# Seven block products instead of eight for the gates and branches of a token-mixer merge

## The chip, the cores and the metric

The kernel runs on one core of a Trainium2 chip. The metric is the device time of one execution in microseconds (us). The kernel before was timed three times: 1023.58, 1023.82 and 1025.4 us, median 1023.82. A further execution was taken by the hardware profiler: 1023.27 us, of which 1021.6 us lie between its first and its last instruction (the span).

Engines are named as in the profile: PE is TensorE (PEld its weight loads), DVE is VectorE, ACT is ScalarE, POOL is GpSimd, SP is SyncE, which issues most DMAs here.

## The reference

One decoder layer over 512 tokens of width 1024, in float32. Cut to what matters:

```python
u = rmsnorm(h, g_mix)
(rq, rk, rv, rgate, dq, dk, dv, dz, db, da, gate_r, gate_d) = split(u @ w_in)
ro = retention(rotary(rq), rotary(rk), rv)            # then normed per head
y_ret = (silu(rgate) * ro) @ w_ret_br                 # 1024 x 1024
do = gated_delta(...)                                 # conv, l2norm, chunked solve, scan; then normed
y_dn = (do * silu(dz)) @ w_dn_br                      # 1024 x 1024
merged = sigmoid(gate_r) * y_ret + sigmoid(gate_d) * y_dn
h = h + merged @ w_o
up = causal_dwconv(rmsnorm(h) @ w_up) + b             # 2 x 2816 columns
a, b = split(up)
h = h + (silu(a) * b) @ w_down
out = rmsnorm(h)
```

The change is about the four matrices of 1024 x 1024 behind `merged`: the two gate parts of `w_in`, `w_dn_br` and `w_ret_br`.

## The kernel before, in words

Every dense product is computed from float32 values that are split in two: a rounded high part (`hi`, type fp32r) and the rest (`lo`). A product is then three matmuls: hi x hi, lo x hi, hi x lo. Weights come from memory in raw blocks of 128 x 1024 floats (512 KB), which SP fetches (`fetch`, DMA lines 232 and 235) into two buffers `wraw`. `weights` then makes the parts: ACT casts the raw block to `whi`, DVE subtracts to get `wlo`. Four pairs of `whi` and `wlo` (`WB = 4`) lie ahead of PE. All engine operations go through a wrapper, so that in the profile every ACT, DVE or POOL operation has line 154, every matmul line 169 and every transpose line 173.

The stages, in order of time:

- **Mixers** (from the start to about 448 us). Dense products of the input rows `u` with the parts of `w_in` (`pk`, `pq`, `pv`, `pr`, `pz`), among which the small products of the mixers are put. The delta mixer has 8 heads in two groups of four. For each group `solve` inverts 64 triangular blocks of 32 x 32: it reads them back from memory (`sa`, line 703), runs 31 steps of two dependent DVE operations each (`xtmp`, `xx`), writes the inverse to memory (`x_dram`) and loads it transposed (`tt`, line 719); PE then builds larger inverses (`pm`) and the scan runs (`psc`). `egb` (line 670) is a row of decays spread over partitions, loaded per head. POOL does small powers (`rsqrt`) for all norms: `rk`, `rq`, `rgn`, `ro`.
- **z gates.** `gate_out` multiplies the mixers' outputs (`roT`, `doT`, transposed: channels on partitions) by a SiLU gate from `pz` and splits them into `rr` and `dd`, 8 tiles of 128 x 512 each.
- **Merge.** For each of 8 channel blocks `c`, PE computes two gates from `u` (`pgate`) and two branches from `dd` and `rr` (`py`), 24 matmuls each (`dense_c`: 8 blocks of depth, three passes); ACT takes the sigmoids; DVE multiplies, adds and splits into `mh`, `ml`, which are already transposed as the next product needs them.
- **`w_o`** (`po`, from 622 us): rows by `dense_r`, residual into `h1`, second norm, transposes (`pt`, line 173).
- **Feed-forward** (`pa`, `pb`, from 668 us), with a convolution over tokens on DVE.
- **Down projection** (`pd`, from 910 us). It is already computed in the form of seven products: the matrix and the activations are cut in quarters, seven sums of quarters are multiplied in place of eight quarter products (Strassen's scheme in Winograd's form), and the results are added. The seven lists of weights need four sums of quarters (`s1` to `s4`). They are made in memory by `presum` on POOL's queue: a DMA copies one quarter to a scratch tensor (line 248), a second DMA adds another quarter to it (line 250, `accum_op=ADD`), 704 KB each, while the feed-forward part runs.

The order of the work on PE, ACT, DVE and POOL is the order in which the program writes the instructions. A small planner (`Order`) sets that order: dense products advance its clock, other work is a set of generators that run when their time has come, with assumed costs for each engine, and `hold` moves the clock until a condition is met. On the chip each engine takes its own list in order and waits only for data and buffers; the planner's times play no part there. SP's list is ordered by the compiler's framework.

```python
P, T, NT, KT, H = 128, 512, 4, 8, 8
PRODUCTS = (("w11", "B11"), ("w12", "B21"), ("s2", "T2"), ("s1", "T1"), ("s3", "T3"), ("s4", "B22"), ("w22", "T4"))
HEAP, HEAP2, RAWB, WB = 64, 17, 2, 4
```

Of the kernel before, what the change touches and what calls it, by code (L numbers as in the profile page):

```python
# [54 lines left out]
KW = NK * 512  # L55
PRODUCTS = (("w11", "B11"), ("w12", "B21"), ("s2", "T2"), ("s1", "T1"), ("s3", "T3"), ("s4", "B22"), ("w22", "T4"))
WD = {"w11": 0, "w12": 1, "w21": 2, "w22": 3}
SUMS = (("s1", "w21", "w22"), ("s2", "w11", "s1"), ("s4", "w12", "s2"), ("s3", "w11", "w21"))


def weight_blocks():
# [12 lines left out]
    for c in range(8):  # L74
        b += [("c", "w_in", GD + c * P), ("c", "w_in", GR + c * P),
              ("c", "w_dn_br", c * P), ("c", "w_ret_br", c * P)]
# [4 lines left out]
    for name, _ in PRODUCTS:  # L81
        b += [("d", name, i, min(2, NK - 2 * i)) for i in range((NK + 1) // 2)]
# [4 lines left out]
NB = sum(b[0] != "d" for b in BLOCKS)  # L87
# [88 lines left out]
def body(nc, tc, ctx, io):  # L176
# [45 lines left out]
    count = dict(fetch=0, split=0, take=0)  # L222

    def fetch():
        i = count["fetch"]
        if i < len(BLOCKS):
            b = BLOCKS[i]
            if b[0] == "d":
                n, own = 512 * b[3], (i - NB) % 4 < 2
                raws[i] = (wp if own else late[0]).tile([P, n], F32, name="wraw" if own else "wraw2",  # L230
                                                        tag="wraw" if own else "wraw2", bufs=RAWB)
                sp.dma_start(raws[i], quarter(b[1])[:, 1024 * b[2]:1024 * b[2] + n])
            else:
                raws[i] = wp.tile([P, D], F32, name="wraw", tag="wraw", bufs=RAWB)
                sp.dma_start(raws[i], io["w"][i])
            count["fetch"] += 1


    sums = {n: dram.tile([P, KW], F32, name=n) for n, _, _ in SUMS}

    def quarter(name):
        return io["wd"][WD[name]] if name in WD else sums[name]

    def presum():
        for n, a, b in SUMS:
            for i in range(4):
                c = ck(i, KW // 4)
                nc.gpsimd.dma_start(sums[n][:, c], quarter(a)[:, c])
                yield 6.0
                nc.gpsimd.dma_start(sums[n][:, c], quarter(b)[:, c], accum_op=ALU.add)  # L250
                yield 8.0

    def weights():
# [6 lines left out]
        raw = raws.pop(i)  # L260
# [7 lines left out]
        yield  # L268
        fetch()
# [46 lines left out]
    def dense_r(pss, x, k0=0, nb=4, last=KT, done=None, groups=(range(NT),), tail=1):  # L316
# [18 lines left out]
        for ts in groups:  # L335
# [4 lines left out]
            for t in ts:  # L340
                for n, part in enumerate(parts[t]):
                    for i in range(nb - tail, nb):
                        block(i, (t,), part)
                        if t == NT - 1 and n == len(parts[t]) - 1:
                            used()
# [761 lines left out]
    def combine(k):  # L1107
# [10 lines left out]
        for n in ("B11", "B12"):  # L1118
            del act_raw[n, k]
# [235 lines left out]
```

## Time and profile before

| what | value | read from |
|---|---|---|
| median of three runs | 1023.82 us | times |
| profiled execution, its own time | 1023.27 us | times |
| its span | 1021.6 us | page |
| granted clock of PE over the span | 0.997 | cores |
| PE busy | 1006.7 us, 99% | page, part 1 |
| DVE busy | 640.6 us, 63% | page, part 1 |
| ACT busy | 463.8 us, 45% | page, part 1 |
| DMA moved | 131.60 MB | page, part 2 |
| chain that ended last | PE 82%, DVE 9%, ACT 4% | page, part 4 |

A row of the profile names its line, engine, operation and tiles (out<-in), the shape, the count, the busy time with the mean in ns, and the idle time of the engine just before it with what ended it. Matmuls overlap one another, so the time from one start to the next says more than a duration. DMA rows give the size of one transfer and the median time from issue to landing.

### The profile page before, as it was taken

What the parts mean: (1) busy time and instruction counts of PE and PEld (TensorE: products, weight loads), DVE (VectorE), ACT (ScalarE), POOL (GpSimd) and SP (SyncE); (2) the same over time, 40 slices, a digit from 0 to 9 for tenths busy, and PEclk for the clock granted to TensorE, in tenths of its full rate; (3) what the DMA queues carried; (4) which work ended last, traced back from release to release, by engine and by line L of the source; (5) the groups of instructions that cost most, each with busy time, mean ns of one, the idle gap of its engine ahead of it and who ended that gap; (6) DMA issues with size and microseconds to landing.
All of it is one profiled execution on the core that took longest, in us unless ns stands there. A gap on an engine that the chain in (4) does not pass through costs nothing.

```text
span 1021.6 us, 13993 instructions
## 1 busy us (share of the span) xinstructions
PE 1006.7 (99%) x5329; PEld 838.5 (82%) x5329; DVE 640.6 (63%) x1224; ACT 463.8 (45%) x956; POOL 77.9 (8%) x100
## 2 busy tenths in 40 slices
PE   8999999999999999999999999999999999999997
PEld 7888778887788886988888888898888888888886
DVE  5777798457777895543333323576655676778785
ACT  5699222475445343742222222444444343356664
POOL 3021100011112000110000000111111000000001
PEclk9999999999999999999999999999999999999999
DMA  5344423211222432094232233368887623246663
GB/s 200 105 119 127 106 83 102 85 64 57 73 74 68 105 111 74 22 282 171 101 103 92 94 103 102 91 195 264 216 240 231 171 100 103 88 129 188 204 189 121
DMA packets 55380, 131.60 MB, mean 129 GB/s; under 512 B 21968, under 2 KB 22288, under 8 KB 55312
## 3 DMA queue, kind: packets, MB, share of 16 engines
q1 hardware_dynamic: 50704, 107.63, 32.8%
q0 software_dynamic: 4608, 23.07, 9.3%
q8 instruction: 42, 0.69, 0.3%
q14 instruction: 26, 0.21, 0.1%
HBM read 127.50 MB, written 26.25 MB: 151 GB/s over the span
## 4 chain that ended last, share of the span: by engine, by line
PE 82%; DVE 9%; ACT 4%; DMA 2%; issue 2%; SPq 1%; POOL 0%; POOLq 0%; DVEq 0%
PE pa L169 12%; PE pb L169 12%; PE pd L169 10%; PE py L169 9%; PE pgate L169 9%; PE pr L169 5%; PE po L169 4%; PE pz L169 4%; PE psc L169 3%; PE pq L169 3%; PE pk L169 2%; DVE wlo L154 2%; PE pv L169 2%; DVE xtmp L154 2%; PE pm L169 2%
## 5 line engine op out<-in xcount | busy, mean ns | idle before, releaser
L154 DVE TENSOR_TENSOR wlo<-wraw,whi 128x1024 fp32r<-128x1024 f32 x182 | 218.6, 1201 | 120.9 <-ACT whi L154 120.4
L154 ACT CAST whi<-wraw 128x1024 fp32r<-128x1024 f32 x182 | 187.9, 1032 | 178.9 <-PE py L169 58.9
L169 PE MATMUL pa<-u2hi,whi 128*128 128x512 f32 (+1 forms) x192 | 71.4, 372 | 0.0
L169 PE MATMUL pa<-u2hi,wlo 128*128 128x512 f32 (+1 forms) x192 | 71.3, 371 | 0.0
L169 PE MATMUL pa<-u2lo,whi 128*128 128x512 f32 (+1 forms) x192 | 71.3, 371 | 0.0
L169 PE MATMUL pb<-u2hi,whi 128*128 128x512 f32 (+1 forms) x184 | 69.9, 380 | 0.0
L169 PE MATMUL pb<-u2lo,whi 128*128 128x512 f32 (+1 forms) x184 | 69.9, 380 | 0.0
L169 PE MATMUL pb<-u2hi,wlo 128*128 128x512 f32 (+1 forms) x184 | 69.9, 380 | 0.0
L154 DVE SCALAR_TENSOR_TENSOR acc<-pb,prm,acc 128x511 f32<-128x511 f32 (+1 forms) x44 | 33.0, 749 | 57.1 <-ACT acc L154 56.4
L169 PE MATMUL pd<-whi,T 128*128 128x512 f32 (+1 forms) x198 | 55.4, 366 | 0.0
L169 PE MATMUL pz<-uhi,whi 128*128 128x512 f32 x128 | 52.6, 411 | 0.0
L169 PE MATMUL pr<-whi,uhi 128*128 128x512 f32 x128 | 52.4, 409 | 0.0
L169 PE MATMUL pz<-uhi,wlo 128*128 128x512 f32 x128 | 50.6, 395 | 0.0
L169 PE MATMUL pz<-ulo,whi 128*128 128x512 f32 x128 | 50.4, 394 | 0.0
L169 PE MATMUL pr<-whi,ulo 128*128 128x512 f32 x128 | 50.0, 391 | 0.0
L169 PE MATMUL pr<-wlo,uhi 128*128 128x512 f32 x128 | 49.9, 390 | 0.0
L169 PE MATMUL pgate<-uhi,whi 128*128 128x512 f32 x128 | 49.8, 389 | 0.0
L169 PE MATMUL pgate<-ulo,whi 128*128 128x512 f32 x128 | 49.8, 389 | 0.0
L169 PE MATMUL pgate<-uhi,wlo 128*128 128x512 f32 x128 | 49.8, 389 | 0.0
L154 DVE SCALAR_TENSOR_TENSOR acc<-pa,prm,acc 128x511 f32<-128x511 f32 (+1 forms) x44 | 33.0, 749 | 19.0 <-ACT acc L154 18.2
L169 PEld LDWEIGHTS pa<-u2hi,whi 128*128 128x128 f32 x192 | 36.2, 189 | 6.3
L169 PEld LDWEIGHTS pa<-u2lo,whi 128*128 128x128 f32 x192 | 36.2, 188 | 6.2
(279 smaller groups left out, 2341.8 us busy)
## 6 DMA issues: line engine op xcount, KB each, us to landing
wraw<-w SPq DMA_DIRECT2D x140, 512.0 KB, 3.5
s<-wd POOLq DMA_DIRECT2D x24, 704.0 KB, 8.3
wraw<-s SPq DMA_DIRECT2D x20, 512.0 KB, 4.2
wraw<-wd SPq DMA_DIRECT2D x15, 512.0 KB, 3.7
s<-s POOLq DMA_DIRECT2D x8, 704.0 KB, 7.2
x<-x SPq DMA_DIRECT2D x8, 256.0 KB, 5.9
gb<-g_dram SPq DMA_DIRECT2D x8, 256.0 KB, 4.0
egb<-e_dram SPq DMA_DIRECT2D x8, 256.0 KB, 3.9
```

The source lines that it names most:

```text
L154: return f(out, *args, **kw)
L169: self.engine.matmul(out, lhsT, rhs, start=start, stop=stop, **kw)
```

## The change

The four matrices of the merge are computed by rows, one after the other (gate of the delta branch, gate of the retention branch, delta branch, retention branch), each in seven products of quarters. Blocks of depth per product are `HK = 4` instead of the 11 of the down projection. Each product has two accumulators of 128 rows x 512 columns and uses two weight blocks of 1024 columns; one weight block now serves 12 matmuls.

What is added: the quarter sums of all four matrices, 16 scratch tensors made by 32 DMAs on POOL's queue (128 x 2048 floats each) that the planner places from its time 40 on, 9.5 apart, in the mixers. Sums of the activations: `combine` makes four quarter sums per tile with four DVE operations of 256 columns; for the input rows POOL first adds `uhi` and `ulo` again. Splits of these operands (`parts_of`, `part_of`) run on ACT and DVE while the matrix before is multiplied, started by product numbers (`since`). Results of some products are copied out of PSUM by ACT (`copied`), others are combined with the copy by DVE (`ended`), then gate and branch are joined (`gate_end`, `branch_end`). Since the merged rows now have tokens on partitions, each of 8 tiles is transposed by PE (`m_out`) and split.

What is removed: the 768 matmuls of the old merge (672 take their place), and the split in `gate_out`, which now leaves its product unsplit. `fetch` may use up to four raw buffers from the merge on (two more in space that the mixers leave). `w_o` takes its first column half in two groups of rows, rows 256 to 511 first. The sums for the down projection are now 16 copies first and then 16 additions, placed 7.0 apart.

```diff
-SUMS = (("s1", "w21", "w22"), ("s2", "w11", "s1"), ("s4", "w12", "s2"), ("s3", "w11", "w21"))
+SUMS = (("s1", "w21", "w22"), ("s3", "w11", "w21"), ("s2", "w11", "s1"), ("s4", "w12", "s2"))
...
+    def presum(s, parts, gap):
+        n = 512 * INNER[s] // parts
+        for add in range(2):
+            for name, a, b in SUMS:
+                for i in range(parts):
+                    c = ck(i, n)
+                    if add:
+                        nc.gpsimd.dma_start(sums[s, name][:, c], quarter(s, b)[:, c], accum_op=ALU.add)
+                    else:
+                        nc.gpsimd.dma_start(sums[s, name][:, c], quarter(s, a)[:, c])
+                    yield gap
...
+    def presums():
+        for s in range(DOWN):
+            yield from presum(s, 1, 9.5)
+    spawn(presums(), 40.0)
...
+    def combine(raw, k, nk, y, z):
+        b11, b12 = halves(raw[k])
+        b21, b22 = halves(raw[k + nk])
+        (t3, t1), (t2, t4) = halves(y), halves(z)
+        vec.tensor_tensor(t3, b22, b12, ALU.subtract)
+        vec.scalar_tensor_tensor(t2, t3, -1.0, b11, ALU.mult, ALU.subtract)
+        vec.tensor_tensor(t1, b11, b12, ALU.subtract)
+        vec.scalar_tensor_tensor(t4, t2, -1.0, b21, ALU.mult, ALU.subtract)
...
     def gate_out(...):
         vec.tensor_tensor(sz, sz, src.pop(c), ALU.mult)
-        hi, lo = S(f"{name}h{c}", F32R), S(f"{name}l{c}", F32R)
-        yield
-        yield from split(hi, lo, sz)
+        raw[c] = sz
...
+    def u_raw():
+        for k in (0, 4, 1, 5, 2, 6, 3, 7):
+            uu[k] = S(f"ur{k}")
+            pool.tensor_tensor(uu[k], uhi[k].bitcast(F32), ulo[k].bitcast(F32), ALU.add)
+            yield 3.0
+            if k >= HK:
+                combine_c(uu, "u", k - HK)
...
-    for c in range(8):
-        for _ in range(2):
-            ps = dense_c(u, "pgate")
-            sg = S2("sg")
-            spawn(sigmoid(sg, ps))
-        for x in (dd, rr_):
-            pys.append(dense_c(x, "py"))
-        spawn(merge(c, sgs, pys))
-    hold(lambda: not order.tasks)
+    def all_operands():
+        yield from operands_c(u_opnd, None, "u", 1.2, (0, 0, 0, 0))
+        yield from operands_c(d_opnd, dd, "d", 2.0, (8, 9, 12, 13))
+        yield from operands_c(r_opnd, rr_, "r", 2.0, (16, 18, 20, 21))
...
+    def m_out(t, i, r):
+        yield 0.2
+        pt = transpose4(r, "pmt")
+        yield
+        hi, lo = S(f"mh{t}{i}", F32R), S(f"ml{t}{i}", F32R)
+        yield from split(hi, lo, pt)
+        mh[t, i], ml[t, i] = hi, lo
...
+    def branch_end(s, t, i, r, ps):
+        g = gates[s - 2].pop((t, i))
+        if ps is None:
+            vec.tensor_tensor(r, r, g, ALU.mult)
+        else:
+            vec.scalar_tensor_tensor(r, ps, -1.0, g, ALU.mult, ALU.mult)
+        if s == 2:
+            merged[t, i] = r
+            return
+        vec.tensor_tensor(r, r, merged.pop((t, i)), ALU.add)
+        yield
+        yield from m_out(t, i, r)
+
+    def matrix(s, opnd):
...
+        A, C = ([PS("py") for _ in range(2)] for _ in range(2))
+        prod(0, [[(full, A[t], True, copied(t, 0, A[t]))] for t in range(2)])
+        prod(1, [[(full, C[t], True, ended(t, 0, C[t], ALU.add))] for t in range(2)])
+        prod(2, [[(full, A[t], False, copied(2 + t, 0, A[t]))] for t in range(2)])
+        E = [PS("py") for _ in range(2)]
+        prod(3, [[(full, E[t], True, copied(2 + t, 1, E[t], -1.0))] for t in range(2)])
+        prod(4, [[(full, A[t], False, ended(2 + t, 1, A[t], ALU.subtract))] for t in range(2)])
+        prod(5, [[(full, E[t], False, ended(2 + t, 0, E[t], ALU.add))] for t in range(2)])
+        prod(6, [[(full, A[t], False, only(t, 1, A[t]))] for t in range(2)], tail=1)
+
+    for s, opnd in enumerate((u_opnd, u_opnd, d_opnd, r_opnd)):
+        matrix(s, opnd)
+    spawn(presum(DOWN, 4, 7.0))
...
-        dense_r([PS("po") for _ in range(NT)], m, done=o_done(i), groups=((0, 1), (2, 3)) if i else (range(NT),))
+        dense_r([PS("po") for _ in range(NT)], m_tile, done=o_done(i), groups=((0, 1), (2, 3)) if i else ((2, 3), (0, 1)))
```

`product` is the loop of the down projection made general: for each weight block and each of two row tiles it issues the three passes, and it starts what follows (`copied`, `ended`, `only`) when the accumulators are complete.

More of the change, by code (lines that the diff above doesn't have):

```diff
@@ L221, in body @@
     raws, ready = {}, {}
-    count = dict(fetch=0, split=0, take=0)
+    count = dict(fetch=0, split=0, take=0, plain=0)
+    free = {"wraw": RAWB, "wraw2": 0}
     def fetch():
-        i = count["fetch"]
-        if i < len(BLOCKS):
-            b = BLOCKS[i]
[L228 to L232, printed above, removed]
-            else:
-                raws[i] = wp.tile([P, D], F32, name="wraw", tag="wraw", bufs=RAWB)
-                sp.dma_start(raws[i], io["w"][i])
-            count["fetch"] += 1
@@ L239, in body @@
[L239 to L251, printed above, removed]
+        while count["fetch"] < len(BLOCKS) and any(free.values()):
+            tag = "wraw" if free["wraw"] else "wraw2"
+            free[tag] -= 1
+            i = count["fetch"]
+            count["fetch"] += 1
+            b = BLOCKS[i]
+            n = 512 * b[4] if b[0] == "q" else D
+            raw = (wp if tag == "wraw" else late[0]).tile([P, n], F32, name=tag, tag=tag, bufs=RAWB)
+            if b[0] == "q":
+                sp.dma_start(raw, quarter(b[1], b[2])[:, 1024 * b[3]:1024 * b[3] + n])
+            else:
+                sp.dma_start(raw, io["w"][count["plain"]])
+                count["plain"] += 1
+            raws[i] = raw, tag
@@ new lines, in body, with quarter @@
+    sums = {(s, n): dram.tile([P, 512 * INNER[s] + 64], F32, name=f"{n}_{s}") for s in range(5) for n, _, _ in SUMS}
+    def quarter(s, name):
+        if name not in WD:
+            return sums[s, name]
+        return (io["wd"] if s == DOWN else io["wm"][s])[WD[name]]
+    def presum(s, parts, gap):
[9 more added lines that the diff above has]
+                    yield gap
@@ L268, in weights @@
         yield
+        free[tag] += 1
         fetch()
@@ L325, in block @@
             whi, wlo = blocks[i]
-            hold(lambda: x[1][k0 + 2 * i + 1] is not None)
+            hold(lambda: all(x(k0 + 2 * i + kk, t) for t in ts for kk in range(2)))
             for t in ts:
@@ L452, in body, with u_tile @@
     u_ready = set()
+    def u_tile(k, t):
+        return uhi[k][:, ck(t)], ulo[k][:, ck(t)]
     def u_split(hf, k, pt):
@@ L1211, in body, with down @@
     done = [0] * NT
[L1213 to L1216 removed]
+    def down(p, accs, tail=0):
         at[0] = p
[L1218 to L1253 removed]
@@ L1264, in fifth @@
+    down(1, [[(full, C[t], True, into(t, 0, C[t], ALU.add, last=True))] for t in range(2)])
+    down(2, [[(full, A[t], False, into(2 + t, 0, A[t], ALU.add))] for t in range(2)])
+    down(3, [[(full, E[t], True, into(2 + t, 1, E[t], ALU.subtract))] for t in range(2)])
     def fifth(t):
```

266 lines of the change are left out of this document (158 added, 108 removed).

## The prediction, made before the changed kernel was run

> **What bounds the kernel now.** I read the page's head first, then busy time by stretches, then the instructions of the merge's tiles, then the waits of TensorE.
>
> ```profile
> span 1021.6 us, 13993 instructions
> ```
>
> PE's busy share has modelled ends and proves little; the instructions of the two merge tiles do. These are the first and the last group of the stage (minimum, median and maximum in ns, then first and last start):
>
> ```profile
> L169 PE MATMUL pgate<-uhi,whi x128: 389/389/389, 448.3 to 610.8; 128*128 128x512 f32 x128
> ```
> ```profile
> L169 PE MATMUL py<-rrh,wlo x64: 389/389/389, 465.1 to 622.1; 128*128 128x512 f32 x64
> ```
>
> Gates and branches are 6 groups of 128 or 64, 768 matmuls in all (3x128 + 6x64). From 448.3 to the last start at 622.1 are 767 steps: 173.8 / 767 = 0.2266 us each. No duration differs from 389 ns, so nothing interrupts the stage: **the matmul count sets its 174 us.** The table by stretches (PE, PEld, DVE, ACT, POOL busy in us with counts, clock, DMA share, GB/s) shows how the other engines stand in it, and in three other stages that matter below:
>
> ```profile
> 120.00:140.00 20.00, 19.32 (x92) 15.14 (x91) 19.55 (x38) 3.15 (x3) 0.00 (x0) 1.00 0.21 68
> ...
> 340.00:360.00 20.00, 20.00 (x90) 16.55 (x89) 19.25 (x40) 7.98 (x11) 0.00 (x0) 1.00 0.31 101
> ...
> 380.00:400.00 20.00, 17.74 (x154) 12.92 (x153) 10.63 (x25) 6.50 (x13) 0.00 (x0) 0.91 0.35 103
> 500.00:520.00 20.00, 20.00 (x90) 16.57 (x89) 6.41 (x8) 5.05 (x7) 0.00 (x0) 1.00 0.31 106
> ...
> 700.00:720.00 20.00, 20.00 (x90) 16.55 (x89) 11.43 (x15) 7.46 (x11) 2.72 (x4) 1.00 0.89 251
> 940.00:960.00 20.00, 20.00 (x90) 16.57 (x89) 17.77 (x31) 13.97 (x28) 0.00 (x0) 1.00 0.62 179
> ```
>
> In the merge (500 to 520) DVE is busy 6.41 of 20 us. In the two triangular solves of the mixers (120 to 140, 340 to 360) it is busy 19.3 to 19.6: there DVE is the scarce engine. The down projection (940 to 960), which already has the form that the merge gets, runs PE at full pace (90 matmuls in 20 us) with DVE at 17.77.
>
> **Part 1, fewer matmuls.** Each of four matrices becomes 7 products of 4 blocks x 2 row tiles x 3 passes, 168 matmuls, so 672 instead of 768. They are of the down projection's shape, whose pace the last row above shows to be the same. 96 x 0.2266 = **21.8 us less**.
>
> **Part 2, new transposes.** The merged rows must be turned before `w_o`: 8 tiles of 4 transposes. The nearest row is in the chain of waits (start, length):
>
> ```profile
> 674.36 1.91 PE pt L173 x16
> ```
>
> 0.12 us each, 32 of them: **3.8 us more**, all on PE. Bounds: 2 (some fall in a wait) to 5.
>
> **Part 3, DVE and ACT in the merge.** Weight blocks rise from 32 to 56, each a cast on ACT and a subtraction on DVE; each now feeds 12 matmuls (2.72 us) instead of 24. Operand splits move here from the z gates, and sums of operands, row ends and signs are new. DVE overlaps neighbours, so I price by start-to-start times, from the timeline of DVE in the down projection:
>
> ```profile
> 925.04 1.22 DVE L154 TENSOR_TENSOR wlo<-wraw,whi 128x1024 fp32r<-128x1024 f32 x1
> 926.18 0.68 DVE L154 TENSOR_TENSOR h<-h,pd 128x512 f32<-128x512 f32 x1
> 926.78 1.22 DVE L154 TENSOR_TENSOR wlo<-wraw,whi 128x1024 fp32r<-128x1024 f32 x1
> 927.91 1.09 DVE L154 TENSOR_TENSOR T<-z,T 128x256 fp32r<-128x256 f32 x3
> 928.92 1.22 DVE L154 TENSOR_TENSOR wlo<-wraw,whi 128x1024 fp32r<-128x1024 f32 x1
> ```
>
> So 1.14 us for 1024 columns, 0.60 for 512, 0.335 for 256. DVE then has 56 weight blocks (63.8), 40 splits of 512 (24.0), 8 of 256 (2.7), 32 quarter sums for the two branches (10.7), 24 combinations with PSUM (14.4), 16 products with a gate (9.6) and 8 additions (4.8): 130 us in a stage of 672 x 0.2266 = 152 us, 86%. On ACT:
>
> ```profile
> L154 ACT CAST whi<-wraw 128x1024 fp32r<-128x1024 f32 x175 | 183.5, 1049 | 173.0 <-PE py L169 58.9 <-PE pr L169 40.9 <-PE pd L169 22.6
> ...
> L154 ACT ACTIVATE sg<-pgate 128x512 f32<-128x512 f32 x16 | 9.6, 598 | 56.9 <-PE pgate L169 56.9
> ```
>
> 56 casts of 1.05, 80 operations of 512 at 0.6, 8 short ones: near 111 us, 73%. Neither exceeds the stage, and the down projection bears 89% of DVE without a wait. But the load is uneven. In the third matrix (the first branch) the operands of the fourth are made as well. At its fifth product, 5.44 us long, DVE gets two weight blocks (2.3 us) and about 2.6 rounds of quarter sums and splits (2.0 us each): 7.5 us. At the sixth, two weights, four row-end operations (2.4) and 1.4 rounds: 7.5. At the seventh, 6.3. The backlog goes 2, 4, 5 us. A weight block may be late by 3 x 2.72 = 8.2 us (four buffers) less cast, subtraction and hand-overs, about 5.4; a PSUM tile that the next matrix reuses must be read within 5.4, and is read after 5 + 1.2. **I take 1.5 us**; bounds 0 (DVE keeps up as at 940) to 6 (11% of idle within DVE's queue, as at 940, over matrices two to four: 107 us of work / 0.89 = 120, against 114).
>
> **Part 4, the hand-over to `w_o`.** Before, the last channel's merge needs four DVE operations. Now `w_o` starts with rows 256 to 511, whose last half ends with product six; only product seven (5.44 us) covers the way: two row tiles each need a combination, a gate product, an addition and a split on DVE (8 x 0.60 = 4.8), two weight blocks pass between them (2.3), the pair of product five leaves 4.8 + 2.3 - 5.4 = 1.7, plus transposes (0.5) and a cast (0.6): 9.9. PE waits up to 4.5 us; without backlog or weights, 0.5. Behind it DVE holds `w_o`'s splits, whose first blocks are ready. A wait also has an after-effect here. TensorE's worst wait in mid-kernel, and the matmuls just after it (start, duration):
>
> ```profile
> PE pm L169 <- DMA tt<-x_dram: 2.3, 2, 1.2
> ```
> ```profile
> 388.16 0.63 PE L169 MATMUL pz<-uhi,whi 128*128 128x512 f32 x1
> 388.59 0.63 PE L169 MATMUL pz<-ulo,whi 128*128 128x512 f32 x1
> ...
> 390.29 0.63 PE L169 MATMUL pz<-uhi,wlo 128*128 128x512 f32 x1
> ```
>
> After 2.3 us of waiting they start 0.43 apart, near half pace, until 390.3 (granted clock 0.91 in that stretch): about 7 x 0.2 = 1.4 us on top. So the hand-over costs 0.5 to 5.9; I take **4**, near the upper end because DVE's queue is full there. [...]
>
> **Part 5, the sums of weights during the mixers.** 32 transfers of 1.05 MB on POOL's queue, 16 of them accumulating. Their price and their neighbours:
>
> ```profile
> q0 software_dynamic: 4608, 23.07, 9.3%
> ...
> wraw<-w SPq DMA_DIRECT2D x140, 512.0 KB, 3.5
> s<-wd POOLq DMA_DIRECT2D x24, 704.0 KB, 8.3
> ...
> egb<-e_dram SPq DMA_DIRECT2D x8, 256.0 KB, 3.9
> ...
> sa<-a_dram SPq DMA_DIRECT2D x4, 128.0 KB, 4.8
> ```
>
> 0.093 x 1021.6 / 23.07 = 4.1 us of all 16 engines per MB, 4.3 per transfer. Weight loads bear this: in the feed-forward part (700 to 720, DMA 0.89) PE holds full pace. What does not is the head of each solve; in the chain of waits stands, at the first:
>
> ```profile
> 109.27 5.01 DMA egb<-e_dram
> ```
>
> `egb` is issued behind `sa`, and DVE waits for it. And POOL's queue runs ahead of its plan, since it waits for data only:
>
> ```profile
> 105.49 1.01 POOL L154 TENSOR_TENSOR rq<-ssqq,mhalf 128x4 f32<-128x4 f32 x1 [1.71 <-DVE ssqq L154]
> ```
> ```profile
> 332.52 1.01 POOL L154 TENSOR_TENSOR rq<-ssqq,mhalf 128x4 f32<-128x4 f32 x1 [5.38 <-DVE ssqq L154]
> 422.96 1.01 POOL L154 TENSOR_TENSOR ro<-mso,mhalf 128x4 f32<-128x4 f32 x1 [89.44 <-DVE mso L154]
> ...
> 436.51 0.76 POOL L248 DMA_DIRECT2D s<-wd  x1
> ```
>
> The last row is a sum of the down projection, whose place in the program is behind the merge's last matmul (622.1); it left 186 us earlier, as soon as POOL's work ahead of it was done. So behind each group's last `rq` the next six to ten sums leave as fast as their dependences allow, and one or two lie beside `sa` and `egb`. Each 1.05 MB in flight can hold a small transfer by up to 4.3 us; half of that, 2, is nearer to what a bulk neighbour does to a weight load. DVE, busy 97%, cannot win it back, and TensorE then waits. First solve 2 (0 to 8); second 1, since the low halves of the eight z gates (8 x 0.60) leave DVE in 340 to 380 but the order of work, planned with DVE's costs, closes up accordingly (from -3.7, the whole present stall of 2.3 + 1.4, to 8). **3 us** together. A sum that waits for the sum before it also holds POOL's small powers queued behind it, 0 to 2 us four times, off the path while dense matmuls are left. [...]
>
> **Part 6, at no cost.** Eight additions on POOL rebuild the input rows; POOL is idle from 333.5 to 423, as the row above shows, and even 1 to 2 us each would fit; without that cover they would delay the first gate operands by up to 16 us. The early sums of the down projection, up to five at about 437, compete with block loads of 0.52 MB per 2.72 us; eight blocks (four split, four raw, 21.8 us) cover that; otherwise 0 to 3.
>
> **Sum.** Against the profiled execution's own 1023.27 us (span 1021.6 and 1.7 around it): -21.8 + 3.8 + 1.5 + 4 + 3 = -9.5, so 1013.8; the median of the runs is 0.55 above the profiled time: **1014.4 us.**
>
> **Rivals.** *Nothing waits* (0.18): DVE keeps up as at 940, the hand-over costs 0.5 and the solves gain or lose little: 1023.8 - 21.8 + 3.8 + 0.5 and -3 to +1, 1003 to 1007. For it: PE's pace at 940; against it: Part 4's arithmetic. *DVE becomes the bound* (0.12): 6 in place of 1.5, hand-over at 5.9: 1020 to 1022, perhaps 1017. Against it: 86% on average. *The solves are starved* (0.12), the other side: transfers of sums beside `sa` and `egb` hold DVE's queue at the head of both solves. With 8 us each: 1023.8 - 21.8 + 3.8 + 1.5 + 4 + 16 = 1027; slower from 12.5 us of loss on. For it: POOL's run-ahead and DVE at 97%; against it: weight loads that live beside two bulk transfers at 700. *The change gives nothing* (0.06): the count falls but every stall comes at its middle and the solves take 12: 1022 to 1026.
>
> **Numbers.** My forecast, 1008 to 1020, has 0.52. About 0.2% (2 us) is what a measurement can tell from no change. Faster than 1021.8: 0.52 + 0.18 + 0.09 = 0.79; within: 0.03 + 0.06 = 0.09; slower: 0.12. The range of 8 in 10 is 1003 to 1025.
>
> **What would show it.** Matmuls of the new merge tiles 0.2266 apart, 672 of them. A wait of 2 to 5 us of PE on the split of the merged rows before the first `po`, with starts 0.43 apart behind it. DVE at 17 or more of 20 us in the third matrix, few waits of PE there. `sa` and `egb` landing in 6 to 8 us instead of 4 to 5. I am wrong if PE waits for weights in the merge, if the solves start over 5 us late, or if the hand-over shows no wait.

## The result, and the profile after

The changed kernel took 1054.26 us (median of four runs, 1053.83 to 1055.54), the kernel before beside it 1023.99: a ratio of 1.0295, 95% interval 1.0277 to 1.0313. It is 30 us slower; 1014.4 had been forecast, with 1003 to 1025 as the range of 8 in 10.

Head of the page and queue table of the changed kernel, and first and last starts of tiles (in this kernel the wrapper's line is 160, every matmul has 175, every transpose 179; SP fetches weights in 243 and 245, POOL issues copies in 267 and accumulating transfers in 265):

```profile
span 1053.8 us, 14233 instructions
...
q0 software_dynamic: 9216, 56.63, 21.5%
```
```profile
L175 PE MATMUL pr<-wlo,uhi x128: 387/389/628, 100.7 to 236.4; 128*128 128x512 f32 x128
L175 PE MATMUL pz<-uhi,wlo x128: 387/389/794, 347.4 to 488.7; 128*128 128x512 f32 x128
L175 PE MATMUL py<-whi,uhi x48: 389/389/389, 489.0 to 559.0; 128*128 128x512 f32 x48
L175 PE MATMUL po<-whi,mh x64: 389/389/628, 648.8 to 699.0; 128*128 128x512 f32 x64
```

The same starts for each kernel (us; the rows above are single ones of a tile's three passes; in the table a first start is that of the first pass, the last `pr` that of the second, the last `pz` that of the third; the first solve runs beside `pr`, the second beside `pz`; kernels are named by the labels of the experiments below):

| kernel | `pr` first, last | `pz` first, last | `po` first | `pa` first | span |
|---|---|---|---|---|---|
| before | 99.4, 217.5 | 328.0, 448.1 | 622.4 | 667.7 | 1021.6 |
| after | 100.4, 236.4 | 347.0, 488.7 | 648.8 | 699.7 | 1053.8 |
| e1, no transfers | 100.3, 218.6 | 329.2, 451.2 | 611.2 | 662.1 | 1015.8 |
| e10, e1 and `w_o` turned | 100.1, 218.4 | 328.9, 450.2 | 608.6 | 655.6 | 1009.2 |
| e9, paced wide | 107.9, 228.3 | 339.8, 461.3 | 623.9 | 670.8 | 1024.5 |
| e11, eight in the merge | 101.9, 225.4 | 344.1, 470.7 | 634.2 | 681.1 | 1034.8 |
| e12, later additions | 101.8, 225.7 | 337.1, 463.7 | 629.4 | 676.3 | 1029.9 |
| e17, 16 transfers | 100.8, 221.0 | 332.4, 454.5 | 641.5 | 688.4 | 1042.0 |
| e18, clear of solves | 107.1, 224.7 | 336.7, 460.9 | 622.7 | 669.6 | 1023.3 |

Before to after: first solve 118.1 to 136.0, middle (last `pr` to first `pz`) 110.5 to 110.6, second solve 120.1 to 141.7, merge (last `pz` to first `po`) 174.3 to 160.1, `w_o` 45.3 to 50.9, the rest 353.9 to 354.1. The mixers lose 40.6 us, merge and `w_o` gain 8.6.

The waits of PE in the changed kernel (total us, times, longest), and landing times of the small loads (KB, median us):

```profile
PE pm L175 <- DMA tt<-x_dram: 10.9, 2, 10.3
PE prqT L179 <- DVE qrot L160: 5.9, 1, 5.9
PE prkT L179 <- DVE krot L160: 5.2, 1, 5.2
PE pz L175 <- DVE wlo L160: 5.0, 1, 5.0
PE pvt L179 <- ACT v L160: 3.2, 1, 3.2
PE po L175 <- DVE ml L160: 3.0, 1, 3.0
...
PE py L175 <- DVE ol L160: 2.5, 2, 1.6
```
```profile
egb<-e_dram SPq DMA_DIRECT2D x8, 256.0 KB, 7.3
...
sa<-a_dram SPq DMA_DIRECT2D x4, 128.0 KB, 11.7
```

Before, the longest such row of the mixers was `tt` with 2.3 us, and `egb` and `sa` landed in 3.9 and 4.8. What lies around the first solve, in the timelines of POOL, SP and DVE (start, duration, in brackets the idle time before and what ended it):

```profile
111.23 1.01 POOL L160 TENSOR_TENSOR rq<-ssqq,mhalf 128x4 f32<-128x4 f32 x1 [1.71 <-DVE ssqq L160]
112.19 0.88 POOL L265 DMA_DIRECT2D s<-s  x1
122.06 0.81 POOL L265 DMA_DIRECT2D s<-s  x1 [8.99 <-DMA s<-s]
122.59 2.36 POOL L267 DMA_DIRECT2D s<-wm  x4
```
```profile
112.02 6.04 SPq L781 DMA_DIRECT2D sa<-a_dram  x2
118.17 3.25 SPq L748 DMA_DIRECT2D egb<-e_dram  x1
...
354.24 11.36 SPq L245 DMA_DIRECT2D wraw<-w  x1
```
```profile
125.60 0.69 DVE L160 TENSOR_TENSOR q<-q,egb 128x512 f32<-128x512 f32 x1 [11.34 <-DMA egb<-e_dram]
```

POOL's queue runs ahead right behind `rq`, as forecast: two sums that accumulate and four copies. `sa` is issued at 112.0, beside the first of them, `egb` behind it at 118.2, and DVE stands 11.3 us for `egb`. At the second solve the issue of one weight load took 11.4 us on SP. All of DVE's waits for small loads, after and then before:

```profile
DVE q L160 <- DMA egb<-e_dram: 26.0, 5, 11.3
DVE xtmp L160 <- DMA sa<-a_dram: 10.1, 1, 10.1
...
DVE ta L160 <- DMA tt<-x_dram: 3.2, 3, 2.7
```
```profile
DVE q L154 <- DMA egb<-e_dram: 5.7, 1, 5.7
DVE ta L154 <- DMA tt<-x_dram: 3.0, 3, 2.5
```

So DVE stands 30 us longer for `egb` and `sa`, the loads at the heads (7.9 of them for three `egb` between 60 and 110 us, the rest at the two solves), and as long as before for `tt`, the load at the ends. PE's wait of 10.3 us for `tt` stands at the end of the second solve, and is the lateness of its head. No transfer of sums leaves from 372 us to the end of the solve, and in the chain of waits there the inverse goes out and comes back fast:

```profile
412.22 3.09 DMA x_dram<-xx
...
416.65 1.66 DMA tt<-x_dram
```

ACT stood long for raw weight blocks (16.6 us before):

```profile
ACT whi L160 <- DMA wraw<-w: 81.2, 17, 12.7
```

### The profile page after: what moved, and what is told of

It is laid out like the page before. It is cut to its first block, busy times and chain, and to the rows that moved or that the text cites. A ratio compares the mean times of both kernels' runs of the same rounds, so it can differ in the third digit from the quotient of the medians.

```text
span 1053.8 us, 14233 instructions
## 1 busy us (share of the span) xinstructions
PE 1003.0 (95%) x5265; PEld 834.3 (79%) x5265; DVE 716.8 (68%) x1344; ACT 510.3 (48%) x1028; POOL 112.2 (11%) x140
## 3 DMA queue, kind: packets, MB, share of 16 engines
q0 software_dynamic: 9216, 56.63, 21.5%
## 4 chain that ended last, share of the span: by engine, by line
PE 77%; DVE 10%; DMA 6%; ACT 3%; SPq 2%; issue 2%; POOL 0%; POOLq 0%; ACTq 0%
PE py L175 12%; PE pa L175 11%; PE pb L175 11%; PE pd L175 10%; PE pr L175 6%; PE pz L175 4%; PE po L175 4%; DMA egb<-e_dram 3%; PE psc L175 3%; DVE wlo L160 3%; PE pk L175 2%; PE pq L175 2%; PE pv L175 2%; DVE xtmp L160 1%; PE pm L175 1%
## 5 line engine op out<-in xcount | busy, mean ns | idle before, releaser
L160 ACT CAST whi<-wraw 128x1024 fp32r<-128x1024 f32 x206 | 213.4, 1036 | 223.8 <-DMA wraw<-w 81.2
L160 DVE TENSOR_TENSOR wlo<-wraw,whi 128x1024 fp32r<-128x1024 f32 x206 | 247.7, 1203 | 55.6 <-ACT whi L160 55.0
L175 PE MATMUL py<-whi,ol 128*128 128x512 f32 x160 | 62.5, 390 | 2.5 <-DVE ol L160 2.5
L175 PE MATMUL py<-whi,oh 128*128 128x512 f32 x160 | 62.7, 392 | 0.3 <-ACT oh L160 0.3
L175 PE MATMUL py<-wlo,oh 128*128 128x512 f32 x160 | 62.3, 390 | 0.0
L175 PE MATMUL pz<-uhi,whi 128*128 128x512 f32 x128 | 54.9, 429 | 0.0
L175 PE MATMUL pr<-whi,ulo 128*128 128x512 f32 x128 | 50.9, 397 | 0.0
L175 PEld LDWEIGHTS pa<-u2hi,wlo 128*128 128x128 f32 x192 | 36.2, 189 | 6.2
```

Source lines behind the costliest of these rows:

```text
L160: return f(out, *args, **kw)
L175: self.engine.matmul(out, lhsT, rhs, start=start, stop=stop, **kw)
```

## The experiments

"Before" runs beside every group; their medians were 1022.8 to 1023.5. Where an interval is given it is of the ratio to these. e2, e3, e4 and e8 were executed once each. e1, e3, e8 and e10 load plain quarters in place of sums: their work is the same, their values are not the reference's.

**1. Whose loss is it?** e1 takes the transfers out, e2 puts them into the kernel before, e3 keeps them but for their bytes.

```diff
 # e1: no transfers; in the merge a plain quarter in place of each sum
-    spawn(presums(), 40.0)
 # e2: the kernel before, with the 32 transfers, whose sums nobody reads
+    spawn(msum(), 40.0)
 # e3: as e1, the 32 transfers kept, 64 of 2048 columns
-    nc.gpsimd.dma_start(sums[s, name][:, c], ...)
+    nc.gpsimd.dma_start(sums[s, name][:, :64], ...)
```

> Leaves out the 32 transfers that make the sums of weights during the mixers; where a sum would be loaded, a plain quarter is loaded instead, so the four matrices are computed from wrong weights, with the same number of loads, splits and matmuls. Theory (the transfers crowd out the loads of the mixers): the last z-gate matmul comes back from 488.7 to 448 +- 4 us, and the time is about 1054 - 40 = 1014 us (1010 to 1018). Rival (the new work on ACT, DVE and POOL in the z gates, and the changed order, make the mixers late): the last z-gate matmul stays beyond 470, the time beyond 1035.

> The kernel before, with only the 32 transfers added at the same places in POOL's queue; nothing reads their sums. Theory (crowding): the mixers end about 40 us later than before's 448.1, the time is about 1060 (1050 to 1070). Rival (z-gate work and order): within 5 us of 1024.

> The changed kernel with all 32 transfers cut to 64 of 2048 columns, and plain quarters loaded in place of the sums (wrong weights, same work). POOL's queue keeps its 32 issues and their order, 1/32 of the bytes move. Theory (bytes crowd out loads): as without sums, 1010 to 1018. Rival (POOL's queue: issue time of the transfers and powers queued behind transfers that wait): still over 1030.

Measured: e1 1017.98 (ratio 0.9964, 0.9946 to 0.9983), e2 1057.11, e3 1019.27. The transfers cost 36.3 us in the changed kernel (1054.26 - 1017.98) and 34 in the kernel before, whose solves lack the new work; with 3% of the bytes they cost 1.3, within the spread of e1 (1017.43 to 1022.61). So it is their bytes, not their issues, and not the z gates. In e2 the loss of 33 us lies in the mixers too (last `pz` at 481.2). The other parts together gain 4.9 us.

**2. Which transfers, and what do they hold up?** e4 puts each sum directly behind its copy. e8 has only six copies, 19% of the bytes, three behind the last `rq` of each group. e5 releases each transfer by a small POOL operation (`tick`) that reads a freshly made weight part, one per weight block, with none near `sa` and `egb`. It was to leave out the ends of the solves too, but the blocks chosen for them (27 to 30, 51 to 53) came after the ends.

```diff
 # e4
+    for name, a, b in SUMS:
+        nc.gpsimd.dma_start(sums[s, name][:, c], quarter(s, a)[:, c])
+        nc.gpsimd.dma_start(sums[s, name][:, c], quarter(s, b)[:, c], accum_op=ALU.add)
 # e8 (no other transfers, plain quarters as in e1)
+    if h % GH == GH - 1:
+        for name in ("s1", "s3", "s2"):
+            nc.gpsimd.dma_start(sums[h // GH, name][:, :2048], quarter(h // GH, "w11"))
 # e5, in weights()
+    QUIET = {*range(14, 19), *range(27, 31), *range(41, 47), *range(51, 54)}
+    if todo and i >= 4 and i not in QUIET:
+        pool.tensor_tensor(tick, lo[:, :4].bitcast(F32), mhalf, ALU.add)
+        todo.pop(0)()
```

> The changed kernel with the 32 transfers in pairs: each copy directly followed by its addition, as the kernel before does for the down projection. All bytes still move; an addition waits for its copy, so at most two to three transfers are in flight where POOL has nothing else to wait for, instead of four to six. If the burst matters (how many are in flight at once): the mixers lose about half, 15 to 25 us of the 40, time 1032 to 1042. If only the bytes matter: 1050 to 1058.

> The changed kernel without the 32 transfers (plain quarters are loaded, wrong weights, same work), but with six copies of 1.05 MB, three issued directly behind the last power of q of each group, that is beside the loads at the head of each solve. 19% of the copied and added bytes. If place decides: 10 to 20 us over the 1018 of the version without sums. If bytes decide: 7 us (6/32 of 37). If only additions hurt: within 2 us.

> The changed kernel with the same 32 transfers, each issued only after a small POOL operation that reads the low part of a freshly split weight block, at most one per block, and none for the blocks split around the heads of the two solves and their ends. All bytes move in the mixers as before, but POOL cannot run ahead. Theory (it is the place and the burst): the mixers lose 0 to 8 us against the version without sums instead of 37, time 1018 to 1028. Rival (the bytes alone cost the time): 1045 to 1057.

Measured: e4 1042.91, e8 1037.72, e5 1048.6 (1.0248, 1.0228 to 1.0268). e8 is the telling one: a fifth of the bytes makes over half of the loss, 19.7 us over e1, when it lies at the heads. e4 gives back 11.3 us with all bytes and the same row length, so it also matters how the transfers follow one another; that may be their number at once or their shifted places. e5 missed its forecast, and its time lies where "the bytes alone" had been expected, which e9 and e18 below refute; in e5 `sa` and `egb` landed in 5.2 us, and other small loads were hit, as its waits of PE show:

```profile
PE pm L175 <- DMA tt<-x_dram: 17.4, 2, 9.1
PE pkt L179 <- ACT k L160: 8.9, 1, 8.9
```

`tt<-x_dram` is the inverse coming back at the end of each solve; here it is late itself (11.6 us at the first solve against 2.9 at most before), with transfers leaving at 183 and 186 us beside it. The wait for `k` is ACT standing 6.7 us for `gb<-g_dram`, near 64 us. So there are three places: `gb` (45 to 75 us), the heads of the solves, and their ends.

**3. The hand-over to `w_o`.** e6 is e5 with the first half of `w_o` taking depth blocks 4 to 7 first, whose operands are ready, and 0 to 3 last. e10 is e1 with the same turn. e7 moves the quarter sums of the two branches from DVE to POOL, on top of e6.

```diff
 # e6, e10
-        b += [("r", "w_o", 2 * i, o) for i in range(4)]
+        b += [("r", "w_o", 2 * i, o) for i in ((0, 1, 2, 3) if o else (2, 3, 0, 1))]
 # e7
-        combine(raw, c, HK, y, z)
+        (combine if x == "u" else combine_pool)(raw, c, HK, y, z)
```

> As the paced version, and in the first half of the output product the depth blocks are taken in the order 4 to 7, then 0 to 3, so that it starts with the merged columns that are ready first. Theory (the wait of 3.0 us on the merged split and the half clock behind it are what the hand-over costs): 3 to 6 us faster than the paced version. Rival (DVE's backlog is what costs, the wait only moves to the second two blocks): within 1 us of it.

> The changed kernel without the 32 transfers (the plain quarter is loaded in place of each sum, so the values of the merge are those of other weights) and with w_o's first half in the turned order: the floor for any placing of the transfers. By the hand-over theory the turned order takes away the wait for the split of the merged rows, 3 us, and the half-clock starts behind it, 1 to 2: 1013 to 1015 against 1018.0 without the turn. If the wait only moves to the second pair of row tiles: 1017 to 1018.

> As the version before (paced, turned), and the quarter sums of the two branch operands are made by POOL, six operations of 256 columns, instead of four on DVE: DVE loses 32 operations, 10.7 us of its load in the second and third matrix. Theory (DVE's full queue in the third matrix causes the waits of 2.5 us there, the half clock behind them and part of the hand-over): 2 to 5 us faster than the version before. Rival (latency of the chain, not load): no difference beyond 1 us, or slower by 1 to 3 if POOL delays the operands.

Measured: e6 1044.17 (1.0198, 1.0171 to 1.0224), e10 1010.87 (0.9891, 0.9864 to 0.9918), e7 1056.36. In both turned kernels the wait for `ml` is gone, and `po` has no half-speed matmuls any more (longest 478 ns in both, 628 in the changed kernel). In e10:

```profile
L175 PE MATMUL po<-whi,mh x64: 389/389/478, 608.6 to 654.9; 128*128 128x512 f32 x64
```

By the table, merge and `w_o` together take 210.9 us in e1 and 205.4 in e10: the hand-over cost 5.5 (7.1 by the medians of e1 and e10, 4.4 by those of e5 and e6). e7, 12 us slower than e6, shows that DVE was not to be relieved that way: PE waited 7.4 us for `ol` instead of 2.5 and 3.7 for `oh` instead of 0.3. Nor did the waits for `ol` have half-speed matmuls behind them, which the theory named: behind the longest of the changed kernel, 1.65 us, the starts are 0.33 and then 0.23 us apart.

**4. Can all 32 be placed?** e9 keeps e6's scheme with quiet blocks at all three places. e11 moves the two transfers still ahead of `gb` and eight others into the merge. e12 lets the last sum of each matrix follow four transfers later. e18 clears both solves, takes matrices in pairs, and lets some blocks release two.

```diff
 # e9
-    QUIET = {*range(14, 19), *range(27, 31), *range(41, 47), *range(51, 54)}
+    QUIET = {*range(7, 10), *range(13, 19), *range(23, 27), *range(41, 46), *range(48, 54)}
 # e11 (e12: also 54, and every fifth block of the merge)
+    SLOTS = {4, 10, 11, 12, *range(19, 23), *range(27, 41), 46, 47, *range(60, 92, 4)}
 # e18
+    SLOTS = {**dict.fromkeys((3, 4, 12, *range(30, 41), 54, 55, 57, 61, 65, 69, 73, 78, 83, 88), 1),
+             **dict.fromkeys((10, 11, 32, 34, 36, 38), 2)}
```

> All 32 transfers stay and are released one per new weight block, as in the two paced kernels before, and w_o's first half takes its depth blocks in the turned order. But now no transfer is released beside any of three kinds of small load that a waiting engine needs at once: gb (blocks 7 to 9), the heads of both solves (13 to 18, 41 to 45) and the x_dram loads at the ends of both solves (23 to 26, 48 to 53). 14 of them leave in the middle region, 220 to 340 us, where the changed kernel carried 14 at no loss. Theory 'it is the place' (a transfer costs only what it holds up of a small load that an engine is waiting for): the mixers give back nearly all, pz ends at 450 to 458 instead of 482.3, and the time is 1012 to 1022, under the kernel before. Rival 'it is the bytes' (each transfer costs about 1 us wherever it lies): 1035 to 1048, as the paced kernels.

> The wider paced kernel before this lost 16 us to the floor without transfers (1010.9): 7.8 of them between 44 and 108 us, where two transfers leave 4 us ahead of g_dram and gb; 2.1 and 1.0 around the first solve's end; 4.1 in the merge, where four transfers left in its first 25 us beside its first weight blocks. Here those two and those four move: 24 transfers stay in the mixers (block 4, blocks 10 to 12, 19 to 22, 27 to 40, 46 and 47), and the last matrix's 8 leave during the merge, one per four weight blocks (10.9 us), where the profile without transfers shows the 16 DMA engines busy 0.56 and weights eight blocks ahead. Theory 'it is the place': 1012 to 1018, below the kernel before (1023.3). Rival 'the merge pays': eight transfers of 4.3 us beside weight loads hold up weights or TensorE there by over 5 us: 1019 to 1027. If the gb wait comes from something else than the two transfers: 1022 or more, with pr again first at 107.

> The kernel before this had the gb wait gone (pr first at 101.9 instead of 107.9), but four sums that accumulate on a sum only just issued stood on POOL's queue for 3.5 to 7.9 us (147, 159, 271, 379 us), with POOL's small powers behind them (TensorE then waited 3.4 for ro), and in the merge eight transfers and the five run-ahead sums of the down projection filled the DMA engines from 520 to 580. Here the last accumulation of each matrix goes four transfers later, so that no transfer waits for the one just before it; 25 transfers stay in the mixers and 7 leave in the merge, one per five weight blocks (13.6 us); the down projection's sums are held until the merge's last blocks. Theory 'place, and POOL's queue behind a waiting sum': first solve back to 120, second to 121, merge 158 to 160: 1014 to 1020. If the queue matters little and the bytes beside the solves decide, the solves keep their 123 and 126: 1024 to 1030.

> All 32 transfers whole (8 KB rows), none now between 100 and 200 us nor between 330 and 420 us: two leave near 30, five at 77 to 90, fifteen between 200 and 325 (four blocks release two), two near 430, and eight in the merge, one per four to five weight blocks. Matrices take turns in pairs, so that no sum follows directly on the one it adds to. Against the last placing of all 32 (1025.2) the first solve should come back from 123.6 to 118 or 119 between the first and last product of its dense stage, the second from 126 to 121, and the merge stay 5 to 7 us above its 146. By 'misplaced transfers' 1013 to 1020, below the kernel before. If the fuller middle (DMA engines some 0.8 busy) now delays gb or POOL's powers there: 1022 to 1030.

Measured: e9 1027.05 (1.0035, 1.002 to 1.0049), e11 1032.95 (1.0096, 1.0069 to 1.0122), e12 1025.19 (1.0015, 1.0004 to 1.0026), e18 1022.47 (0.999, 0.9979 to 1.0001). Place, order and turn are worth 32 us at equal bytes, from 1054.3 to 1022.5, some 4 to 7 of them by the turn. But each forecast below the kernel before was missed, and e18 cannot be told from it. e9 lies between its two theories. e11 did take the loss ahead of the first `pr` away (101.9 instead of 107.9), so the two transfers ahead of `gb` were its cause. It lost 8 us in the middle (118.7), where one accumulating transfer stood 7.9 us on POOL's queue at 271 us, 5 in each solve (123.5 and 126.6), and 5 in the merge, with eight transfers in it (163.5 against 158.4 in e10). e12 took the loss in the middle away (111.4); its solves stayed (123.9 and 126.6), as its rival had it, and so did its merge (165.7). The profiles of e12 and e18 are of their slowest executions, 6.5 and 2.6 us above the medians. What e18 still loses against e10 is 14.1 us of span: 7.0 before the first `pr`, 1.5 in the middle, 2.9 in the second solve, 3.3 in merge and `w_o`. Some of its stretches and a wait (columns as in the prediction), and the first `pr` of e12:

```profile
80.00:100.00 20.00, 20.00 (x104) 16.86 (x103) 14.68 (x26) 15.32 (x38) 5.65 (x9) 1.00 1.00 277
100.00:120.00 20.00, 17.64 (x86) 14.71 (x85) 9.13 (x19) 11.26 (x36) 3.69 (x5) 0.91 0.75 209
...
400.00:420.00 20.00, 18.41 (x176) 14.82 (x175) 9.81 (x29) 7.64 (x29) 0.00 (x0) 0.83 0.12 44
```
```profile
PE pkt L179 <- ACT k L160: 2.4, 1, 2.4
```
```profile
L175 PE MATMUL pr<-whi,uhi x128: 389/389/775, 101.8 to 225.4; 128*128 128x512 f32 x128
```

Two blocks released two transfers each near 80 to 90: the DMA engines stand at 1.00 there, PE loses 2.4 us in the next stretch, and its clock falls from 1.00 to 0.91; e12, with three transfers there instead of five, reaches `pr` 5.3 us earlier. About 1 of these 5.3 was there by 69 us, where e18 had one transfer more near 30 (`pk` at 68.7 against 67.6). The first solve itself is then free of loss (117.6). In 400 to 420 no transfer runs (DMA 0.12), and PE still lost: at 402.0 it had waited 1.6 us for ACT's copy of `tt` (0.9 in e10), and that stretch's clock is 0.83. What makes ACT late there is not settled.

**5. How does a transfer hold up a small load?** e13 and e14 are the changed kernel with each transfer cut along its columns into four or eight, so rows of 2 and 1 KB in place of 8 KB.

```diff
-            yield from presum(s, 1, 9.5)
+            yield from presum(s, 4, 2.375)
```

> The changed kernel with each of the 32 transfers cut along its columns into four, each of 128 rows of 2 KB instead of 8 KB: same bytes, same place in the program, four times the issues on POOL (0.55 us each, 53 us more of an idle POOL). Theory 'whole rows in turn' (a small load waits at each of its packets for a whole row of a transfer): sa and egb land in about half the time, 6 to 8 us instead of 11.7 and 9, and the loss of 37 us shrinks by half or more: 1030 to 1042. Rival 'bytes ahead' (a small load waits for what is already queued, whatever its cut): 1050 to 1060, landing times as in the changed kernel. If short rows make the transfers themselves dearer (more than 4.3 us of all engines per MB): above 1060.

> The same with eight pieces of 1 KB rows (224 more issues on POOL). 'Whole rows in turn': sa and egb at 5 to 6 us and 1025 to 1036, below the kernel with 2 KB rows. 'Bytes ahead': 1050 to 1065.

Measured: e13 1039.89 (1.0153, 1.0116 to 1.019), e14 1054.32 (1.0294, 1.0257 to 1.0331). Landing of `egb` and `sa`, e13, e14, and e4 with its rows of 8 KB:

```profile
egb<-e_dram SPq DMA_DIRECT2D x8, 256.0 KB, 4.8
sa<-a_dram SPq DMA_DIRECT2D x4, 128.0 KB, 8.2
```
```profile
egb<-e_dram SPq DMA_DIRECT2D x8, 256.0 KB, 5.1
sa<-a_dram SPq DMA_DIRECT2D x4, 128.0 KB, 6.2
```
```profile
egb<-e_dram SPq DMA_DIRECT2D x8, 256.0 KB, 5.1
...
sa<-a_dram SPq DMA_DIRECT2D x4, 128.0 KB, 7.4
```

The median of the four `sa` loads goes from 11.7 to 8.2 to 6.2 with the row length, as "whole rows in turn" says. That does not show it. The pieces leave POOL mostly 0.5 to 4 us apart, so less may have been in flight beside `sa` as well, and e4 gets 7.4 with whole rows. Nor does it hold solve by solve: at the first, `sa` lands in 9.8 us in the changed kernel (4.4 before), 10.9 in e13, 6.0 in e14, 8.1 in e4; at the second in 16.3 (5.4 before), 7.3, 7.2 and 6.4. Row length and the number of transfers in flight were not separated. e13's time is where "whole rows in turn" had it, e14's where "bytes ahead" had it: in e14 the first solve takes 136.7 us, as long as in the changed kernel, and the middle 121.7; POOL is busy for 228 of the first 450 us with its 256 issues (149 in e13), and PE waits elsewhere (5.7 us for ACT's `v`, 4.3 for `q`). That the one makes the other was not tried. e15 and e16 put e12's placing and 2 KB rows together, e16 with the four transfers nearest to the solves moved to the middle.

```diff
+            for j in range(4):
+                c = ck(j, 128 * INNER[s])
                 nc.gpsimd.dma_start(sums[s, name][:, c], quarter(s, q)[:, c])
```

> The last paced kernel (1025.2, profiled at 1031.7) with each transfer cut into four of 2 KB rows, issued back to back at its slot. If place and row length add up: the solves and the merge give back half of what they still lose there (5.6, 5.2 and 7 us): 1014 to 1021, below the kernel before. If four issues in a row on POOL cost as much as the short rows save: 1023 to 1030.

> The same, with the four transfers that leave next to the solves (at about 137, 141, 360 and 365 us) moved to the middle of the mixers (four of its blocks release two). If what is left of the loss in the solves comes from these: first solve 118 to 119 and second 121 between first and last matmul of their dense products, 2 to 6 us below the other kernel of this pair: 1012 to 1018. If the middle then overflows (DMA engines at 0.75 there already): gb or weights late between 220 and 340, and no gain.

Measured: e15 1051.63, e16 1081.67: far off both theories. The middle is the place (143 us in e15 and 161 in e16, instead of 110). POOL's and DVE's timelines there in e15, and the wait of PE:

```profile
260.73 0.81 POOL L278 DMA_DIRECT2D s<-wm  x1 [5.42 <-issue]
261.28 1.33 POOL L160 TENSOR_TENSOR rgn<-rvar,mhalf 128x4 f32<-128x4 f32 x1
...
272.41 2.60 POOL L278 DMA_DIRECT2D s<-s  x3 [0.31 <-issue]
279.59 0.81 POOL L278 DMA_DIRECT2D s<-s  x1 [4.59 <-issue]
```
```profile
262.65 1.37 DVE L160 TENSOR_SCALAR ro<-pro,mv,rgn 128x128 f32<-128x128 f32 x4 [9.32 <-POOL rgn L160]
```
```profile
PE proT L179 <- DVE ro L160: 14.8, 4, 8.4
```

Three accumulating pieces leave some 0.9 us apart; the fourth stands 3.7 to 5.4 us, and POOL's power `rgn`, queued behind it, comes late; DVE waits 9.3 us for it, PE for DVE. Four copied pieces leave in 2.1 to 2.4 us without standing. That is the second price of these transfers: a queue in order, shared with small operations on the path.

**6. Only 16 transfers.** e17 makes `s1` and `s2` in memory, at places that had cost nothing so far, and `s3` and `s4` by the load itself: SP loads one summand, an accumulating transfer adds the other into the raw block.

```diff
+    sp.dma_start(raw, quarter(b[1], x)[:, c])
+    nc.gpsimd.dma_start(raw, quarter(b[1], y)[:, c], accum_op=ALU.add)
 # and
+    SLOTS = {10, 11, 12, *range(27, 40)}
```

> 16 transfers instead of 32: only s1 and s2 of each matrix are made in memory, paced, at the places that cost nothing so far (blocks 10 to 12, near 80 to 95 us, and 27 to 39, near 220 to 330). s3 and s4 are made by the load itself: SyncE loads the one summand into the raw block, and a transfer on POOL's queue adds the other to it there, 16 of 0.5 MB in the merge, where the DMA engines were busy 0.56 and weights are eight blocks ahead. w_o is turned. Theory 'the loss is the misplaced transfers': mixers as without transfers (pz last at 450 to 455), merge within 3 us of the 157 there: 1011 to 1017, below the kernel before by 6 to 12 us. If the adding loads come too late in the merge (two loads in a row, the second on a queue that waits): TensorE waits for weights there, 1018 to 1030. If 16 well-placed transfers still cost half of what 32 do: 1024 to 1029.

Measured: 1044.03 (1.0204, 1.0183 to 1.0225). The mixers did what "misplaced transfers" says: last `pz` at 454.5, 4.3 us behind e10 with half of all transfers. The merge did not: 187.0 us instead of 158.4. Four adding loads follow each other, each waiting for its first load (POOL stood up to 6.3 us for one); only four raw blocks lie ahead; ACT stands for them, and its other work behind:

```profile
ACT whi L160 <- DMA wraw<-wm: 21.1, 5, 10.0
```

## Why the prediction was wrong

**Part 1 held.** Where nothing waits, 90 matmuls start in 20 us, as before:

```profile
600.00:620.00 20.00, 20.00 (x90) 16.53 (x90) 19.77 (x28) 12.49 (x17) 0.00 (x0) 1.00 0.69 211
```

From the last `pz` to the first `po` pass 160.1 us; the old 174.3 less 21.8, with 3.8 and 1.5 for transposes and waits, had been 157.8, and the first part of the hand-over lies in it.

**Part 2 held.** In e10's timeline a group of four transposes puts 0.36 us between two matmuls, and the step behind it is 0.08 longer: eight groups make 3.5, against 3.8 taken. e10's merge and `w_o`, 205.4 against 219.6 before, leave 2.3 us for all that was not counted in Parts 1 to 3.

**Part 3 held in size.** In e1 the third matrix runs from 527 to 565 us. DVE is busy 17.93 of 20 us within it and 19.80 across its end, and PE does not wait there; 2.5 us of waits for `ol` follow early in the fourth, against 1.5 taken (0 to 6):

```profile
540.00:560.00 20.00, 20.00 (x90) 16.56 (x89) 17.93 (x31) 11.56 (x17) 0.00 (x0) 1.00 0.57 198
560.00:580.00 20.00, 20.00 (x90) 16.58 (x89) 19.80 (x28) 12.26 (x16) 0.00 (x0) 1.00 0.56 191
```

**Part 4: right mechanism, size near the edge.** PE waited 3.0 us for `ml`, and from 1.2 us behind that wait six matmuls of `po` took 0.63 us each and started 0.43 apart (0.39 and 0.23 before it); the turn in `w_o` took both away and gave 5.5 us. Taken were 4, bounds 0.5 to 5.9.

**Part 5 is the step that failed.** Its 3 us measured 36.3. The mechanism was named (POOL's queue runs ahead, one or two sums lie beside `sa` and `egb`, DVE waits and cannot win it back), and the rival *The solves are starved* is what happened, at more than twice its price. The term that was mis-sized is what a transfer does to a small load, and three things were wrong in it.

First, one transfer of 1.05 MB was taken to hold a small load by at most the 4.3 us that its bytes take of all engines, and half of that was chosen from what bulk does to weight loads; both were the author's estimates. At the first head, beside one sum issued with it, `sa` landed in 9.8 us instead of 4.4, `egb` in 7.4 instead of 5.0, and SP took 6.0 us instead of 2.9 for the two issues of `sa`, behind which `egb` stands. At the second, beside up to three, `sa` landed in 16.3 instead of 5.4 and `egb` in 9.0 instead of 3.9. The delays add up along this chain, and DVE stood 36 us for these two loads instead of 6. What in a transfer does this was not shown: `sa` landed in 11.7, 8.2 and 6.2 us at rows of 8, 2 and 1 KB (the changed kernel, e13, e14), but the runs do not separate the row length from the number of transfers in flight. The rival was weighed and set at a chance of 0.12, since weight loads bear bulk at 700. That row does not carry over: in the kernel before, the feed-forward part has two raw buffers as the mixers have, each addition waits there for its copy (POOL stood 56.1 us before six of them from 700 to 760), the DMA engines are at 0.89, and blocks landed in 4.8 us (median of 700 to 760, 8.2 at most); from 120 to 160 us in the changed kernel the DMA engines are at 1.00 and over.

Second, only `sa` and `egb` were counted; weight blocks beside them were left out (ACT stood 81.2 us for them instead of 16.6, and PE once 5.0 for `wlo` in `pz`). The ends of the solves were left out too, but they cost nothing extra here, only in e5, where transfers lay at them.

Third, the long waits have the after-effect that Part 4 counted for `w_o` and Part 5 did not. In the changed kernel PE's waits for `qrot` (5.9 us), `krot` (5.2), `wlo` (5.0) and `tt` (10.3) are followed by 5, 7, 12 and 13 matmuls that take 0.63 us or more and start 0.43 apart for the most part; the stretch 400 to 420, with the wait for `tt`, was granted a clock of 0.78.

```profile
400.00:420.00 20.00, 9.10 (x51) 7.16 (x50) 16.15 (x36) 4.13 (x5) 3.62 (x1) 0.78 0.34 99
```

The bound of 8 us per solve was thus no bound: it was 18 and 22. The forecast of what would show it, `sa` and `egb` in 6 to 8 us, was half right: `egb` took 7.3, `sa` 11.7.

**Part 6 held**: the eight additions on POOL run from 375 to 458 us, beside the second solve, which without transfers (e1) takes 122.0 us instead of 120.1, and the first gate matmul starts 0.3 us behind the last `pz`.

The sum, redone with what was measured: -8.7 for merge and `w_o` (e1's 210.9 against 219.6), +3.1 for the mixers without transfers, -0.2 for the rest, +36.3 for the transfers: +30.5, and 30.3 it was.

Open: what the last 11.6 us between e18 and e10 (1022.47 and 1010.87) would take. Some 4 of them go with the five transfers near 80 to 90, by comparison with e12; what in a transfer holds up a small load is open as well; whether 32 can be placed without loss was not shown, and no kernel here that computes the reference is measurably faster than the one before.

## What to carry to other kernels

Price a bulk transfer that "runs in idle DMA time" less by its bytes than by the small loads that an engine waits for at that moment (e8: a fifth of the bytes, 19.7 of 36.3 us of loss): list every such load (here `gb`, `sa`, `egb`, `x_dram`) with its time before placing one. POOL's queue did not keep the plan's times (of transfers planned 9.5 us apart six left within 12.8 us, from 112.2 to 125.0): tie each transfer to something that happens where you want it (a small operation reading a fresh tile did it here), and count what stands behind it on that queue (in e15 DVE waited 9.3 us for `rgn`). Where a stage begins with operands of the last product, start it with those that are long ready (5.5 us here, e10 against e1).

## What was not expected of the hardware

- SP's own issues were held up in the changed kernel: `sa`'s two at the first solve took 6.0 us (2.9 before) and that of one weight load 11.4 (0.3 for most), and what SP issued next started behind them, `egb` at 118.2 and 365.6 us.
- Short rows made the transfers dearer for the engines. For the same 56.6 MB the software queue takes 21.5% of 1053.8 us in the changed kernel and in e14, with 1 KB rows in the mixers, 26.5% of 1052.3:

```profile
q0 software_dynamic: 29184, 56.64, 26.5%
```

- A late weight block did not cost the same everywhere. Between 110 and 170 us, with two raw buffers, the blocks of the changed kernel landed in 8.2 us (median; up to 13.2) and ACT stood 5 to 9 us for single ones; in the feed-forward part (700 to 800), with four, they landed in 8.9 and PE kept full pace. That the buffers make the difference was not tried.
